# Splitting the contraction of a tuned fp32r feed-forward's up products into two 64-row matmuls with PSUM banks of their own

## The chip, the core and the metric

The kernel runs on one core of one Trainium2 chip. The metric is the device time of one launch in microseconds, the median of three runs. All TensorE work of the feed-forward layers is in fp32r; the six engines that the profile names are PE (matmuls), PEld (the weight loads of PE), DVE (VectorE), ACT (ScalarE), POOL (GpSimd) and SP (SyncE, which here only issues DMAs).

## The reference, cut to what matters

A trunk of two layers over 512 tokens of width 1024. Layer 0 mixes tokens with an RG-LRU, layer 1 with an S5 block; each mixer is followed by a gated feed-forward with a causal convolution of three taps over the tokens. The second of these two feed-forwards is the place of the change:

```python
D_MODEL, SEQ, D_FF, FFN_CONV_W = 1024, 512, 3072, 3

def _conv_ffn(h, w_up, conv_w, conv_b, w_down):
    up = _causal_dwconv(h @ w_up, conv_w, conv_b)
    return (jax.nn.gelu(up[..., :D_FF]) * up[..., D_FF:]) @ w_down

# in reference(), for each layer i
hn = _rmsnorm(h, norm_ffn_g[i])
h = h + _conv_ffn(hn, ffn_w_up[i], ffn_conv_w[i], ffn_conv_b[i], ffn_w_down[i])
```

`h @ w_up` is [512 x 1024] by [1024 x 6144]: 48 tiles of 128 output channels, each contracted over 8 chunks of 128 input channels. All values are float32.

## The kernel before, in words

Channels lie on partitions and tokens on the free axis, so a tile is [128 channels, 512 tokens]. Each float32 operand is kept as a rounded high part and a remainder, both fp32r, and a product of two chunks is three matmuls ("passes") into one PSUM bank: high by high, high by remainder, remainder by high (`mm3`, L213 to L217). Each pass is a weight load of 128 rows by 128 columns and a matmul of 128 rows by 512 columns.

The work is a stream of jobs. A job is one weight tile of [128, 1024] (512 KB): a DMA on SP's queue (L176), its high part by ACT (L188 through L211), its remainder by DVE (L189 through L199), and then 24 passes on PE. `run` (L120) emits jobs in order: two jobs ahead the weight is split, five ahead it is loaded; three raw buffers and three split buffers rotate. What follows a product is put off by `defer` to a later job, at a phase ahead of the weight split (0), behind it (1), ahead of the products (2) or behind them (3).

In the feed-forward (`ffn`, L378) there are six parts of four channel tiles. `up(p)` makes eight tiles, four that go through the gelu (a) and four that gate (g); `down(p - 1)` follows it with four jobs. The order is up(0), up(1), down(0), up(2), down(1), and so on, with down(5) at the end in a form of its own (`final`, L1306), where the products have 256 columns. Of the 48 up tiles the first four (the a tiles of up(0)) go through `group` (L239), contraction outermost; the other 44 go through `product` (L229), contraction innermost, which is 24 passes into one bank, taken by `bank()`. There are two PSUM pools of four banks each, A and B. Up products use A, except for the g tiles of up(0), which use B as the down products do.

One job after a tile's products, `half` (L390) evicts it: `conv_a` (L361) multiplies the bank by the row of 1/rms into a padded buffer on DVE (L363, recorded at L199) and makes the last tap and the bias on ACT (L364, recorded at L211); `conv_b` adds the two other taps on DVE (L368, recorded at L208). Then the gelu on ACT (a tiles), or a product on DVE, a rounded copy on ACT and the remainder on DVE (g tiles).

```python
def mm3(self, ps, wh, wl, xh, xl, start, stop):            # L213
    mm(ps, wh, xh, start=start, stop=False)                # L215
    mm(ps, wh, xl, start=False, stop=False)                # L216
    mm(ps, wl, xh, start=False, stop=stop)                 # L217

def conv_a(self, ps, pad, taps, bias, cv):                 # L361
    self.tt(pad[:, n - 1:n - 1 + S], ps, self.rb, MUL)
    self.act(cv, pad[:, n - 1:n - 1 + S], AF.Identity, scale=taps[n - 1], bias=bias)
```

In the trace the names are those of the tiles: `pa` and `pb` are banks of A and B, `ah` and `al` the parts of the second feed-forward's input, `nh` and `nl` those of its gated activations, `whi` and `wlo` those of the weights.

Of the kernel before, what the change touches and what calls it, by code (L numbers as in the profile page):

```python
# [20 lines left out]
S = 512          # tokens  # L21
D = 1024         # model width
KD = D // P      # chunks of channels
FF = 3072
FP = 4           # ffn chunks in one part
# [3 lines left out]
L = 8            # tokens of one step of the chunked S5 scan  # L29
# [3 lines left out]
NGC = P // GC    # groups in one chunk of channels  # L33
# [20 lines left out]
class Job:  # L54
    """One weight tile's worth of matrix products (or, without src, only a place in the order). The weights
    come as [128, 1024], of which a row is split into a parts; cut: pieces that are loaded and split apart."""
# [10 lines left out]
WARM = 8        # matrix products that raise the clock of the tensor engine before the first data is there  # L67
AHEAD = 2        # jobs between the split of a weight and its use
BG = 5.1         # the vector engine's budget for one job, work in the background included (see cost)


class Trunk:
    def __init__(self, tc, ctx):
# [27 lines left out]
        self.sgn = c.tile([P, 2], F32, name="sgn")   # (+1 top, -1 bottom), (-1 top, +1 bottom)  # L101
# [4 lines left out]
        self.imod = c.tile([P, GC], F32, name="imod")  # 1 where column = partition mod 16  # L106
        self.h = [self.hp.tile([P, S], F32, name=f"h{k}") for k in range(KD)]

# [1 line left out]
    def defer(self, ticks, phase, fn, cost=0.0):  # L110
        """Emit fn that many jobs later; phase 0 before the weight split, 1 after it, 2 before the products,
        3 after them."""
        self.queue.setdefault((self.t + ticks, phase), []).append((fn, cost))
# [54 lines left out]
    def load(self, j, part=None):  # L168
        """DMA of a job's weights, or of one of its pieces."""
        if j.raw is None:  # L170
            j.raw = self.wraw.tile([P, 1024], F32, tag="raw", name="raw")
            j.left = list(range(j.cut))
        n = 1024 // j.cut
        for _ in range(len(j.left) if part is None else 1):
            i = j.left.pop(0)
            self.nc.sync.dma_start(out=j.raw[:, i * n:(i + 1) * n], in_=j.src[:, i * n:(i + 1) * n])  # L176

    def split_weight(self, j, part=None):
        """hi and lo of a job's weights, or of one piece."""
# [38 lines left out]

    def pair(self, role):
        """(hi, lo) tiles of a norm's output (role 0) or of what follows it (role 1); the two pools change  # L220
        roles when self.turn does."""
# [7 lines left out]
    def product(self, w, c, x, bank, post):  # L229
        """128 columns of w^T x (tile c of w, c > 3), contraction innermost; x() gives its (hi, lo) lists."""  # L230
        def emit(wh, wl):
            ps = bank()
            xh, xl = x()
            for k in range(KD):
                self.mm3(ps, wh[:, k, :], wl[:, k, :], xh[k], xl[k], k == 0, k == KD - 1)
# [3 lines left out]
    def group(self, w, x, bank, post):  # L239
        """The first 512 columns (tiles 0 to 3 of w), contraction outermost, so that the last chunks of x may  # L240
        come late."""
# [19 lines left out]
    def norm_begin(self, gain):  # L261
        """gain(k): column of gains for chunk k, or None for the last norm."""
# [3 lines left out]
    def norm_act(self, k):  # L266
        """hi of h * g, squares."""
# [15 lines left out]
    def norm_vec(self, k):  # L283
        """lo of h * g, sum of the squares."""
# [14 lines left out]
    def norm_rsqrt(self):  # L299
        """1/rms of every token as [128 tokens, 4]."""  # L300
# [14 lines left out]
    def norm_bcast(self):  # L315
        """1/rms of the tokens on every partition."""
# [4 lines left out]
    def spread(self, ps, t, r):  # L321
        """Column t of r, a value per token, as a row on every partition."""
# [8 lines left out]
    def norm_tail(self, d=0):  # L331
        """The rest of the norm, spread over the jobs of the next phase's first group."""
# [5 lines left out]
    def residual(self, m, ps, view=lambda h, ps: (h, ps), norm=True, d=1):  # L338
        """h[m] += ps as a post of the running job, with the next norm's part for this chunk."""
# [21 lines left out]
    def conv_a(self, ps, pad, taps, bias, cv):  # L361
        n = len(taps)
        self.tt(pad[:, n - 1:n - 1 + S], ps, self.rb, MUL)  # L363
# [14 lines left out]
    def ffn(self, w_up, w_down, ft, next_gain, before_last=None, last=None):  # L378
# [4 lines left out]
        def half(ps, f, d, then):  # L383
            """conv of one 128-channel tile; then(cv) right behind it."""
# [41 lines left out]
        def up(p):  # L426
# [6 lines left out]
            for f in fs:  # L433
                if p:
                    yield self.product(w_up, f, self.x_now, self.bankA,
                                       lambda ps, f=f: half(ps, f, 1, a_half(f)))
                yield self.product(w_up, FF // P + f, self.x_now, self.bankA if p else self.bankB,
                                   lambda ps, f=f: half(ps, FF // P + f, 1, g_half(f)))
# [31 lines left out]
    def project(self, w, x, next_gain, view=lambda h, ps: (h, ps), turn=0, mid=None):  # L470
        """h += w^T x; mid is emitted half way."""
# [12 lines left out]
    def rglru(self, x, g_first, late_tables, gt, w_in, w_a, w_x, w_out, next_gain, then):  # L484
# [30 lines left out]
        def four(tag, c):  # L515
            """Slice c of a tile for four chunks, whose transcendental functions then are one instruction."""
# [159 lines left out]
    def exp_parts(self, pool, x, n, pre):  # L676
        """x (overwritten, clamped) -> expm1 of the reduced argument, k of 2^k."""
# [16 lines left out]
    def softplus_neg(self, tmp, lam):  # L694
        """-2 and -4 times softplus(-lam) over [128, 8]."""
# [4 lines left out]
        self.ts(v, lam, -1.0, 0.0, op0=MUL, op1=ALU.max)       # max(-lam, 0)  # L700
        self.stt(z, v, -2.0, lam, MUL, SUB)                    # -2 max(-lam,0) - lam = -|lam|
# [3 lines left out]
        self.stt(p, p, 1.0, e, ADD, MUL)                       # exp(-|lam|)  # L705
# [16 lines left out]
    def s5_pre(self, a, log_dt, b, c, d_col):  # L722
        """Matrices and tables of the chunked scan, one chunk of 8 groups at a time, into DRAM: a list of
        (emit, cost on the vector engine). Partitions hold (real | imaginary) x state unless said otherwise."""
        nc, tc = self.nc, self.tc
        G = NG
        self.d_P = self.dr.tile([KD, P, 2304], F32, name="d_P")     # S, four tables of e, R
# [10 lines left out]
        def open_tab():  # L738
            st["tab"] = ExitStack()
            tab = st["tab"].enter_context(tc.tile_pool(name="s5tab", bufs=1))  # L740
            for n in ("pw_r", "pw_s", "pw_n", "pw_m"):   # Re lambda^k, +-Re, -Im, -+Im
# [44 lines left out]
        def s_theta():  # L786
            # theta = ai dt, reduced, halved
# [22 lines left out]
        def s_w():  # L810
            cm, co, si, sn, cs = t("cm"), t("co"), t("si"), v["sn"], v["cs"]
            self.stt(cm, sn, -2.0, sn, MUL, MUL)           # cos - 1
# [5 lines left out]
            # w = (lambda - 1) conj(a) / |a|^2  # L818
# [17 lines left out]
            self.ts(t("wis"), wi, self.sgn[:, 1:2])        # -wi top, +wi bottom  # L836
            # rho8 = mag^8
# [6 lines left out]
        def power_block(re, im, base, lo, n, tmpn):  # L844
            """entries lo+1..lo+n = entry(base) * entries 1..n"""
# [36 lines left out]
        def unit_square():  # L882
            # squares e^{i x}, kept at modulus 1
# [14 lines left out]
        def s_e1t():  # L898
            pi8 = v["pi"][:, :, 0:8]
            power_table(v["e1c"], pi8, v["co"], v["si"], 7)  # L900
            self.ts(v["e1s"], pi8, self.sgn[:, 1:2])       # -sin top, +sin bottom

        def s_e2t():
            e2, e2x = v["e2"], v["e2x"]
            power_table(e2, e2x, v["co"], v["si"], 7)
            # e2 = cos top, sin bottom; e2x = sin top, cos bottom
# [13 lines left out]
        # Bbar and its swapped halves  # L920
# [72 lines left out]
        def c_K(m, R):  # L993
            # K[(l, c), (g, c')], then [(g, c'), (l, c)]
# [58 lines left out]
        def t_move():  # L1053
            # T_g[(j', c'), (j, c)] = K_{j - j'}[c', c]
# [19 lines left out]
    def s5(self, w_in, w_glu, w_out, next_gain):  # L1074
# [19 lines left out]
        def tables(c):  # L1094
            # e^{i 8 theta n}: [cos; sin], then [cos; cos] and [sin; sin]
# [12 lines left out]
        def params2(c):  # L1108
            # the first chunks' matrices wait in tiles that the activations need only later
# [15 lines left out]
        def up(c, ps):  # L1125
            # rows of a chunk are (c, g); tokens in (j, n) order, then to [(j, c), (g, n)] through DRAM
# [397 lines left out]
```

## Time and profile before

| what | value |
|---|---|
| median of 3 runs | 1209.42 us (1209.22 to 1210.38) |
| profiled execution, from its first to its last instruction | 1204.7 us |
| what the median has beyond that span | 4.7 us |
| PE busy | 1190.3 us, 99% of the span, 5616 matmuls |
| PEld busy | 992.3 us, 82% |
| DVE busy | 887.1 us, 74% |
| ACT busy | 525.9 us, 44% |
| mean granted TensorE clock | 0.993 of full speed |

A profile shows when each engine executed something. PE's durations run from a matmul's start to its modelled end and overlap one another, so the step from one start to the next tells what a matmul costs in a stream. The profile states no separate whole time for the profiled execution; its span is set beside the median of the runs.

### The profile page before, as it was taken

To read this page: it belongs to the slowest core of one execution; us is meant where nothing else is said; L and a number is where in the kernel's file an instruction comes from. 1 tells how busy PE (TensorE), PEld (TensorE's weight loads), DVE (VectorE), ACT (ScalarE), POOL (GpSimd) and SP (SyncE) were. 2 spreads that over 40 slices of the span, in tenths; PEclk is the share of its full clock that TensorE was granted. 3 is DMA by queue.
4 is the path that set the end of the run, shared out by engine and by line. 5 is a ranking of instruction groups with operands and counts; after the bars stand their busy time and mean duration, and the time that the engine had idled before them with its cause. 6 is when DMAs were issued, how large, how long until landed. Compare 5 with 4: busy or idle time off the path is not lost.

```text
span 1204.7 us, 14706 instructions
## 1 busy us (share of the span) xinstructions
PE 1190.3 (99%) x5616; PEld 992.3 (82%) x5616; DVE 887.1 (74%) x1469; ACT 525.9 (44%) x711; POOL 18.6 (2%) x35
## 2 busy tenths in 40 slices
PE   9999999999999999999999999999999999999997
PEld 7777888888888888888889888888888888888886
DVE  7899799989989888678597432657766757575765
ACT  5588425424334243436267342524433434242434
POOL 0000000000000000102001000000000000000000
PEclk9999999999999999999989999999999999999998
DMA  7212423247553443457377522223232222223212
GB/s 271 85 56 88 143 88 105 97 121 272 169 159 125 143 142 125 130 192 272 116 217 250 163 99 100 93 95 98 89 104 91 101 95 98 100 92 105 89 70 71
DMA packets 78439, 154.15 MB, mean 128 GB/s; under 512 B 26464, under 2 KB 42224, under 8 KB 78240
## 3 DMA queue, kind: packets, MB, share of 16 engines
q1 hardware_dynamic: 74256, 138.26, 34.8%
q0 software_dynamic: 4112, 14.94, 3.4%
q8 instruction: 44, 0.72, 0.2%
q14 instruction: 27, 0.22, 0.1%
HBM read 131.69 MB, written 23.86 MB: 129 GB/s over the span
## 4 chain that ended last, share of the span: by engine, by line
PE 92%; DVE 4%; ACT 2%; DMA 1%; issue 1%; SPq 0%; DVEq 0%; ACTq 0%
PE pa L215 17%; PE pa L217 17%; PE pa L216 17%; PE pb L215 12%; PE pb L217 12%; PE pb L216 12%; PE py L1184 1%; PE py L1183 1%; PE kps L998 1%; PE pv L1142 1%; DVE wlo L199 1%; PE sps L1033 1%; DMA raw<-in_rg_w_in_dram 1%; DVE xc L208 0%; PE rb L323 0%
## 5 line engine op out<-in xcount | busy, mean ns | idle before, releaser
L211 ACT ACTIVATE whi<-raw 128x1024 fp32r<-128x1024 f32 (+1 forms) x201 | 211.6, 1054 | 372.0 <-PE pa L216 164.0
L199 DVE TENSOR_TENSOR wlo<-raw,whi 128x1024 fp32r<-128x1024 f32 (+1 forms) x201 | 244.7, 1218 | 93.6 <-ACT whi L211 82.1
L215 PE MATMUL pa<-nh,whi 128*128 128x512 f32 x520 | 207.6, 400 | 0.7 <-ACT whi L211 0.7
L217 PE MATMUL pa<-nh,wlo 128*128 128x512 f32 x520 | 202.8, 391 | 0.1
L216 PE MATMUL pa<-nl,whi 128*128 128x512 f32 x520 | 202.3, 389 | 0.0
L215 PE MATMUL pa<-ah,whi 128*128 128x512 f32 x448 | 173.9, 391 | 1.4 <-DVE g L199 1.4
L216 PE MATMUL pa<-al,whi 128*128 128x512 f32 x448 | 174.5, 390 | 0.0
L217 PE MATMUL pa<-ah,wlo 128*128 128x512 f32 x448 | 174.4, 389 | 0.0
L208 DVE SCALAR_TENSOR_TENSOR cv<-pad,t_f,cv 128x512 f32<-128x512 f32 x192 | 142.5, 748 | 3.6 <-ACT cv L211 1.8
L215 PE MATMUL pb<-nh,whi 128*128 128x512 f32 (+1 forms) x344 | 129.0, 375 | 0.0
L217 PE MATMUL pb<-nh,wlo 128*128 128x512 f32 (+1 forms) x344 | 127.8, 371 | 0.0
L216 PE MATMUL pb<-nl,whi 128*128 128x512 f32 (+1 forms) x344 | 127.7, 371 | 0.0
L215 PE MATMUL pb<-ah,whi 128*128 128x512 f32 x320 | 125.4, 392 | 0.0
L217 PE MATMUL pb<-ah,wlo 128*128 128x512 f32 x320 | 124.6, 390 | 0.0
L216 PE MATMUL pb<-al,whi 128*128 128x512 f32 x320 | 124.5, 389 | 0.0
L199 DVE TENSOR_TENSOR pad<-pa,rb 128x512 f32<-128x512 f32 x88 | 60.7, 690 | 78.2 <-PE pa L217 78.0
L199 DVE TENSOR_TENSOR h<-h,pb 128x512 f32<-128x512 f32 (+1 forms) x112 | 72.3, 648 | 61.6 <-PE pb L217 61.2
L215 PEld LDWEIGHTS pa<-nh,whi 128*128 128x128 f32 x520 | 97.6, 188 | 22.5 <-issue 1.7
L217 PEld LDWEIGHTS pa<-nh,wlo 128*128 128x128 f32 x520 | 97.5, 188 | 21.8 <-DVE wlo L199 0.9
L216 PEld LDWEIGHTS pa<-nl,whi 128*128 128x128 f32 x520 | 97.7, 188 | 21.2 <-issue 1.7
L215 PEld LDWEIGHTS pa<-ah,whi 128*128 128x128 f32 x448 | 83.9, 188 | 18.8 <-DVE g L199 1.8
L217 PEld LDWEIGHTS pa<-ah,wlo 128*128 128x128 f32 x448 | 84.1, 188 | 17.6
(280 smaller groups left out, 1488.8 us busy)
## 6 DMA issues: line engine op xcount, KB each, us to landing
raw<-in_ffn_w_up_dram SPq DMA_DIRECT2D x96, 512.0 KB, 3.5
raw<-in_ffn_w_down_dram SPq DMA_DIRECT2D x48, 512.0 KB, 3.5
raw<-in_s_w_glu_dram SPq DMA_DIRECT2D x16, 512.0 KB, 3.5
raw<-in_rg_w_in_dram SPq DMA_DIRECT2D x15, 512.0 KB, 3.4
mS<-d_P SPq DMA_DIRECT2D x8, 640.0 KB, 5.9
raw<-in_rg_w_out_dram SPq DMA_DIRECT2D x8, 512.0 KB, 3.5
d_T<-zero POOLq DMA_DIRECT2D x1, 4096.0 KB, 16.4
d_P<-se SPq DMA_DIRECT2D x16, 256.0 KB, 2.0
```

What stands on the lines that cost most here:

```text
L199: self.last_vec = self.nc.vector.tensor_tensor(out=out, in0=a, in1=b, op=op).ins
L208: self.nc.vector.scalar_tensor_tensor(out, a, s, b, op0, op1)
L211: self.nc.scalar.activation(out, a, func, **kw)
L215: mm(ps, wh, xh, start=start, stop=False)
L216: mm(ps, wh, xl, start=False, stop=False)
L217: mm(ps, wl, xh, start=False, stop=stop)
L998: nc.tensor.matmul(ps[:, g * GC:(g + 1) * GC], R[:, g, 0:8].rearrange("p l c -> p (l c)"), bst[:, g], start=True, stop=True)
L1033: nc.tensor.transpose(ps[:, i * P:(i + 1) * P], Sm[:, i].rearrange("p l c -> p (l c)"), self.ident)
L1142: nc.tensor.matmul(pv[:, g * NCH:(g + 1) * NCH], mS[:, g * P:(g + 1) * P], us[:, g * NCH:(g + 1) * NCH], start=True, stop=True)
L1183: nc.tensor.matmul(o, mT[g // 4][:, gs], us[:, g * NCH:(g + 1) * NCH], start=True, stop=False)
L1184: nc.tensor.matmul(o, mR[g // 4][:, gs], hs[:, g, 0:NCH], start=False, stop=True)
```

## The change

The 44 tiles of the second feed-forward that go through `product` are contracted in two halves. Each pass becomes two matmuls, one over partitions 0 to 63 and one over partitions 64 to 127, each with its own weight load of 64 rows by 128 columns and its own PSUM bank. A tile takes two banks in place of one. At the eviction ACT copies the first bank into `cv`, DVE adds the second bank to it, and the multiplication by the row of 1/rms reads `cv` in place of PSUM. The order of jobs, the loads and everything in the first feed-forward stay as they are. (The diff also drops comments and docstrings from the file; these hunks are left out.)

```diff
+    def mm3_rows(self, pss, wh, wl, xh, xl, start, stop):
+
+        for q, (w, x) in enumerate(((wh, xh), (wh, xl), (wl, xh))):
+            for ps, r in zip(pss, (slice(0, 64), slice(64, 128))):
+                self.nc.tensor.matmul(ps, w[r], x[r], start=start and q == 0, stop=stop and q == 2)
+
...
-    def product(self, w, c, x, bank, post):
+    def product(self, w, c, x, bank, post, rows=False):
         def emit(wh, wl):
-            ps = bank()
+            ps = (bank(), bank()) if rows else bank()
+            mm3 = self.mm3_rows if rows else self.mm3
             xh, xl = x()
             for k in range(KD):
-                self.mm3(ps, wh[:, k, :], wl[:, k, :], xh[k], xl[k], k == 0, k == KD - 1)
+                mm3(ps, wh[:, k, :], wl[:, k, :], xh[k], xl[k], k == 0, k == KD - 1)
             post(ps)
         return Job(w[c], emit, KD)
...
     def conv_a(self, ps, pad, taps, bias, cv):
         n = len(taps)
+        if type(ps) is tuple:
+            self.act(cv, ps[0], AF.Copy)
+            self.tt(cv, cv, ps[1], ADD)
+            ps = cv
         self.tt(pad[:, n - 1:n - 1 + S], ps, self.rb, MUL)
         self.act(cv, pad[:, n - 1:n - 1 + S], AF.Identity, scale=taps[n - 1], bias=bias)
...
-    def ffn(self, w_up, w_down, ft, next_gain, before_last=None, last=None):
+    def ffn(self, w_up, w_down, ft, next_gain, before_last=None, last=None, rows=False):
...
                 if p:
                     yield self.product(w_up, f, self.x_now, self.bankA,
-                                       lambda ps, f=f: half(ps, f, 1, a_half(f)))
+                                       lambda ps, f=f: half(ps, f, 1, a_half(f)), rows)
                 yield self.product(w_up, FF // P + f, self.x_now, self.bankA if p else self.bankB,
-                                   lambda ps, f=f: half(ps, FF // P + f, 1, g_half(f)))
+                                   lambda ps, f=f: half(ps, FF // P + f, 1, g_half(f)), rows)
...
         yield from K.ffn(ffn_w_up[1], ffn_w_down[1], Taps(1), None,
-                         last=lambda w, x: K.final(w, x, lambda k: gt("fin", k), out))
+                         last=lambda w, x: K.final(w, x, lambda k: gt("fin", k), out), rows=True)
```

## Rows read from the trace of the kernel before

**Rows 1.** The page's first part: engine, busy us, share of the span, instructions

```profile
PE 1190.3 (99%) x5616; PEld 992.3 (82%) x5616; DVE 887.1 (74%) x1469; ACT 525.9 (44%) x711; POOL 18.6 (2%) x35
```

**Rows 2.** The page's chain of work that ended last, by engine

```profile
PE 92%; DVE 4%; ACT 2%; DMA 1%; issue 1%; SPq 0%; DVEq 0%; ACTq 0%
```

**Rows 3.** Busy time by stretch: length, then each engine's busy us (instructions), granted clock

```profile
1169.09:1181.97 12.88, 12.88 (x109) 12.87 (x108) 6.91 (x16) 6.45 (x16) 0.00 (x0) 1.00 0.01 1
842.69:886.21 43.52, 43.52 (x193) 36.04 (x192) 32.34 (x41) 20.02 (x25) 0.00 (x0) 1.00 0.29 97
820.93:842.69 21.76, 21.76 (x97) 18.02 (x96) 19.99 (x28) 11.52 (x17) 0.00 (x0) 1.00 0.30 97
1103.81:1147.33 43.52, 43.52 (x193) 36.04 (x192) 29.12 (x36) 18.17 (x22) 0.00 (x0) 1.00 0.28 97
```

**Rows 4.** Groups of instructions in 1103.81 to 1147.33: count | busy us, mean ns | idle before

```profile
L216 PE MATMUL pa<-al,whi 128*128 128x512 f32 x64 | 24.9, 389 | 0.0
...
L216 PEld LDWEIGHTS pa<-al,whi 128*128 128x128 f32 x64 | 12.0, 188 | 2.5
...
L199 DVE TENSOR_TENSOR pad<-pa,rb 128x512 f32<-128x512 f32 x7 | 4.8, 689 | 8.9 <-PE pa L217 8.9
...
L199 DVE TENSOR_TENSOR h<-h,pb 128x512 f32<-128x512 f32 x1 | 0.7, 686 | 2.0 <-PE pb L217 2.0
```

**Rows 5.** Timeline of PE and PEld at 850 us: start, us, instruction

```profile
850.40 0.39 PE L216 MATMUL pa<-al,whi 128*128 128x512 f32 x1
850.40 0.19 PEld L217 LDWEIGHTS pa<-ah,wlo 128*128 128x128 f32 x1
850.63 0.39 PE L217 MATMUL pa<-ah,wlo 128*128 128x512 f32 x1
850.63 0.19 PEld L215 LDWEIGHTS pa<-ah,whi 128*128 128x128 f32 x1
```

**Rows 6.** Timeline of PEld at 661 us, ten weight loads merged: S5 products of 64 columns

```profile
661.12 1.31 PEld L1142 LDWEIGHTS pv<-us,mS 128*128 128x128 f32 x10
662.35 0.19 PEld L1183 LDWEIGHTS py<-us,mT 128*128 128x128 f32 x1
```

**Rows 7.** Copies of a whole PSUM bank by ACT: min/median/max ns, first and last start

```profile
L211 ACT ACTIVATE us<-pa x8: 578/598/601, 697.6 to 733.0; 128x512 f32<-128x512 f32 x8
```

**Rows 8.** Timeline of DVE from 853 to 859.5 us

```profile
853.77 0.69 DVE L199 TENSOR_TENSOR pad<-pa,rb 128x512 f32<-128x512 f32 x1 [1.54 <-PE pa L217]
854.69 1.22 DVE L199 TENSOR_TENSOR wlo<-raw,whi 128x1024 fp32r<-128x1024 f32 x1 [0.22 <-ACT whi L211]
855.83 1.53 DVE L208 SCALAR_TENSOR_TENSOR cv<-pad,t_f,cv 128x512 f32<-128x512 f32 x2
857.40 0.69 DVE L199 TENSOR_TENSOR ge<-ge,cv 128x512 f32<-128x512 f32 x1
858.79 0.69 DVE L199 TENSOR_TENSOR nl<-ge,nh 128x512 fp32r<-128x512 f32 x1 [0.70 <-ACT nh L211]
```

**Rows 9.** Who waited for whom from 842.69 to 1169.09 us: total us, times, longest

```profile
DVE pad L199 <- PE pa L217: 50.2, 24, 3.3
ACT whi L211 <- PE pa L216: 41.7, 39, 4.4
```

**Rows 10.** Timeline of PE where a down block ends and an up block begins

```profile
1103.59 0.39 PE L217 MATMUL pb<-nh,wlo 128*128 128x512 f32 x1
1103.81 0.39 PE L215 MATMUL pa<-ah,whi 128*128 128x512 f32 x1
```

## The prediction, made before the changed kernel was run

> **What bounds the kernel now.** I read the busy shares first, then the chain of waits, then the second feed-forward by stretches, and last single matmuls on the timeline. PE is busy for 99% of the span [rows 1] and makes 92% of the chain that ended last [rows 2]: what TensorE's stream gains or loses, the kernel gains or loses, and other engines count only where they make PE wait. In the stretches of the change PE has no gap at all at a granted clock of 1.00 [rows 3]. The changed passes lie in 820.93 to 842.69 (the g tiles of up(0), 96 passes) and in five stretches like 842.69 to 886.21 (192 passes each, the last is 1103.81 to 1147.33): 96 + 5 x 192 = 1056 passes, which is 44 tiles of 24.
>
> A pass costs 43.52 us / 192 = 226.7 ns from start to start [rows 3]; the 389 ns of a matmul's row and the 188 ns of a load's [rows 4] are longer because they overlap. The timeline shows how: the load for the next pass starts in the same moment as the running matmul, and the next matmul starts 0.23 us later [rows 5]. At the level of 2.4 GHz, which a granted clock of 1.00 stands for, 512 columns take 213.3 ns, so 13.4 ns of each pass are not columns. The last products, of 256 columns, take 12.88 us / 108 = 119.3 ns [rows 3]; 106.7 ns of it are columns, so the rest is 12.6 ns: a fixed price of some 13 ns per load and matmul, not a slower stream. All that splitting could win on PE is this remainder, for every pass still streams 512 columns through both halves of the array. 1056 x 13.4 ns = 14.2 us is the most, a reason that excludes a larger gain.
>
> The Trainium skill, page "TensorE: Matmul & The Clock Gate", Part 3, section "What overlaps and what doesn't", says that a weight load overlaps matmuls in flight only when it goes to other rows of the array. Here loads of all 128 rows run beside matmuls of all 128 rows [rows 5], so the "only" does not hold in this trace; at most the 13 ns could be what such a load can't hide. Taken at its word, the rule would hide them in the changed kernel, which is the first rival below.
>
> **The change part by part.**
>
> *The passes.* A pass becomes two loads and two matmuls of 64 rows each. No row of the trace has a matmul of fewer than 128 rows, so I bound the price. From below: both row tiles stream together and nothing else shows, 213.3 ns, -14.2 us over 1056 passes. From above: they never run together, each costs what a pass costs now, 2 x 226.7 = 453.4 ns, +239.4 us. Between them lie three rows. If each row tile is a stream of its own with the step of today's passes, and the two streams run side by side, a pass stays at 226.7 ns: no change. If the loads go one after the other: ten loads for matmuls of 64 columns take 1.23 us, from 661.12 to 662.35 [rows 6]; the first step is that of the 512-column matmul still running, 0.23 us [rows 5], so the nine others are (1.23 - 0.23) / 9 = 0.111 us each, and two loads fit into 222 ns, just inside a pass. And if the fixed 13.4 ns is paid for each load and matmul in turn although the columns run together, a pass is 213.3 + 26.8 = 240.1 ns, +14.2 us; twice the step of the 256-column products, 238.6 ns, says the same in another way [rows 3].
>
> I take 226.7 ns. It is the row nearest in kind: the same load of 128 columns beside the same stream of 512, with the weights of the next pass loaded behind the columns of this one, only with each stream's rows halved. Two streams in different rows, with different partitions of the operands and different banks, share no operand and no result in the program. Sum of this term: 0.
>
> *The borders.* Ten times PE passes between split and whole products: into the first stretch, five times out to a down block, four times back. Today such a border costs nothing: the step over it is 0.22 us [rows 10]. If the array has to empty at a border, the price is the tail of a matmul beyond its step, 389 - 227 = 162 ns [rows 4], so 0 to 1.6 us in all. I take 1.0, nearer to the tail since nothing in the trace changes the shape of the array.
>
> *The eviction.* Added per tile: an ACT copy of a bank, 0.60 us [rows 7], and a DVE addition of a bank, 0.69 us as for the residual [rows 4]. 44 x 0.60 = 26 us of ACT and 44 x 0.69 = 30 us of DVE, none of it on PE. The multiplication by 1/rms reads SBUF in place of PSUM; its 0.69 us [rows 4] is the same as that of the gated product, which reads SBUF [rows 8], so 0. DVE's load in a usual up stretch goes from 29.12 to 29.12 + 8 x 0.69 = 34.6 of 43.52 us, in the first one from 32.34 to 37.9; in 820.93 to 842.69 three of the split tiles are evicted, 19.99 + 2.1 = 22.1 us against 21.76 [rows 3]. There alone DVE falls behind, by some 0.3 us and the waits for ACT's copy, and the next stretch has 5.6 us to spare. What hides the eviction is the idle time that DVE now spends waiting for PE ahead of it, 50.2 us in all, and ACT's wait ahead of the weight split [rows 9]. If that cover were gone, 44 x 0.69 = 30 us would lie on PE.
>
> *The wait that is added.* In front of DVE's addition stands ACT's copy, and behind it in DVE's queue are the multiplication, the weight's remainder and the taps; behind the copy in ACT's queue is the next weight's high part. Today the multiplication starts 0.2 us after the tile's end and the remainder 0.9 us after that [rows 8]. Both move by some 1.4 us. The weight so split is used two jobs (10.9 us) later and the gated activations from four jobs later on, so nobody on PE waits for them.
>
> *The banks.* A tile takes two of a pool's four banks, so a pair must be free again after one job of 5.44 us (43.52 / 8). It is free at 0.2 + 0.60 + 0.69 = 1.5 us, plus DVE's arrears. 3.9 us are left: 0. Loads from memory and SP's queue are the same.
>
> **Sum.** 0 + 1.0 + 0 + 0 = +1.0 us on the profiled span of 1204.7 us; the median lies 4.7 us above that span, and with the same difference it becomes 1209.4 + 1.0 = 1210.4 us.
>
> **The rivals.** *The fixed price is hidden.* The load of one half passes while the other half streams, so the 13.4 ns vanish. For it: it is a price per load and matmul, not per column. Against it: loads already run wholly beside columns. It gives 213.3 to 222 ns a pass, the upper end being two loads in turn: -14.2 to -5.0 us, and with the borders 1195.3 to 1206 us.
>
> *The fixed price is paid twice.* 240.1 ns a pass, +14.2 us, with the borders 1224 to 1225 us; with an arrear of DVE of a few us on top up to 1229. For it: it comes once per load and matmul, and their number doubles. It decides if it sits where instructions are taken up one after the other, and not in the array.
>
> *The two halves do not run together*, so the change doesn't do what it is built on. Place: PE's queue, at the second matmul of each pass. Price: 226.7 ns per pass, +239.4 us, 1449 us. It decides as soon as the second half's matmul starts over 0.11 us after the first's and the next pass starts only behind both. For it: every matmul in this trace starts when the one before has streamed, and a matmul of half the rows still has 512 columns. Against it: the program gives no reason for one half to wait for the other.
>
> The Trainium skill, page "TensorEngine Tiling (Array Packing)", section "Key Properties", says that row tiles load and multiply independently and that a change of tiling drains the array. By it this last rival falls and the border's price stands; no run here has shown either yet.
>
> **How the numbers follow.** No change: 0.36, the likeliest, with 1209.4 to 1211.0 as its own range. Price hidden: 0.24. Price paid twice: 0.20. Halves one after the other: 0.20, since nothing in the trace has shown two matmuls at once. A measurement of this kernel can tell 0.2% (2.4 us) from no change. So faster 0.24, same 0.36, slower 0.20 + 0.20 = 0.40. The range takes in the first three cases with their bounds, 1196 to 1229 us, and leaves out the last.
>
> **What would show it.** Right: in a stretch of an up block, 192 passes of two matmuls each in 43.5 us; matmuls of 64 rows whose starts come in pairs or interleave at half a pass; PE without gaps; DVE's pad rows now behind ACT's copy, DVE at 34 to 38 us per stretch; ten short gaps at the borders. Price hidden: the stretch shrinks to 41 to 42.6 us. Paid twice: 46 us. One after the other: 87 us, with a step of 227 ns from each matmul to the next. I am wrong about the eviction if PE's first matmul of a tile waits for ACT or DVE.

## The result, and the profile after

The changed kernel takes 1243.62 us (median of 4 runs, 1238.99 to 1247.12) against 1209.32 us for the kernel before in the same sessions: 1.0292 times, 95% interval 1.0258 to 1.0326. It was forecast at 1210.4 us, no change, with a range of 1196 to 1229. The profiled execution has a span of 1237.2 us in a run of 1238.99 us, the fastest of the four.

The page of the changed kernel, its engines and its chain by engine, set beside [rows 1, 2]:

```profile
PE 1201.5 (97%) x6672; PEld 995.7 (80%) x6672; DVE 915.3 (74%) x1513; ACT 545.1 (44%) x755; POOL 18.6 (2%) x35
...
PE 75%; DVE 15%; ACT 6%; issue 2%; DMA 1%; SPq 0%; DVEq 0%; ACTq 0%
```

1056 more matmuls and loads are there (6672 - 5616), and yet PE's busy time grew by 11 us only. The chain of work that ended last moved: DVE and ACT make 21% of it where they made 6%. By stretches (length, then PE, PEld, DVE, ACT and POOL busy us, granted clock, DMA share, GB/s), beside [rows 3]:

```profile
817.87:839.78 21.91, 21.91 (x193) 19.03 (x194) 17.46 (x25) 11.26 (x17) 0.00 (x0) 1.00 0.24 73
839.78:897.14 57.36, 48.95 (x387) 40.02 (x383) 39.58 (x52) 23.80 (x34) 0.00 (x0) 0.94 0.25 74
897.14:919.15 22.01, 22.01 (x98) 17.94 (x97) 16.72 (x22) 7.67 (x11) 0.00 (x0) 1.00 0.37 118
919.15:967.89 48.74, 45.66 (x385) 36.42 (x384) 30.35 (x39) 19.51 (x27) 0.00 (x0) 1.00 0.25 77
```

The g tiles of up(0) cost what they cost (21.91 us for 21.76), and a down block 22.01 for 21.76. The five other up stretches had 43.52 us each; the first now has 57.36, and the other four have 48.74 to 48.76. From the first split tile to the 256-column products the kernel before needs 1169.09 - 820.93 = 348.16 us and this one 1202.11 - 817.87 = 384.24 us, +36.1 us. This length I use for all runs below: what lies ahead of it differs by some us from run to run of the same code.

PE's timeline in such a stretch, and its loads, beside [rows 5]:

```profile
922.02 0.39 PE L223 MATMUL pa<-ah,whi 64*128 64x512 f32 x2
922.25 0.39 PE L223 MATMUL pa<-al,whi 64*128 64x512 f32 x2
...
922.03 0.19 PEld L223 LDWEIGHTS pa<-al,whi 64*128 64x128 f32 x2
```

The two halves run together: a pair of matmuls starts every 0.23 us, the step that one whole pass had, with two loads beside it. So the passes are as forecast; the 5 us per stretch are lost between tiles. Who waited for whom from 817 to 1202 us (total, times, longest), beside [rows 9]:

```profile
ACT cv L211 <- DVE pad L199: 97.8, 45, 4.2
DVE wlo L199 <- ACT whi L211: 60.7, 49, 4.5
...
DVE cv L208 <- ACT cv L211: 34.6, 44, 0.9
...
PE pa L223 <- DVE cv L199: 14.8, 21, 0.9
...
PE pa L223 <- ACT cv L211: 5.8, 6, 4.6
```

PE waits for DVE's addition (`cv` at L199) and ACT's copy, which is to wait for a pair of banks. In its timeline at the start of a tile, the first half's matmul runs alone, for its bank is free when ACT has copied it; the second half's bank waits for the addition:

```profile
947.00 0.40 PE L223 MATMUL pa<-ah,whi 64*128 64x512 f32 x1
948.27 0.50 PE L223 MATMUL pa<-ah,whi 64*128 64x512 f32 x1 [0.88 <-DVE cv L199]
```

DVE's eviction of the up tiles no longer waits for PE; it waits for ACT, and ACT for DVE. The timeline of DVE over two tiles, beside [rows 8], and under it ACT's over one, show why (start, duration, engine, line, tiles; in brackets the wait ahead and what ended it):

```profile
933.58 0.68 DVE L199 TENSOR_TENSOR cv<-cv,pa 128x512 f32<-128x512 f32 x1
934.29 0.69 DVE L199 TENSOR_TENSOR pad<-cv,rb 128x512 f32<-128x512 f32 x1
935.86 1.54 DVE L208 SCALAR_TENSOR_TENSOR cv<-pad,t_f,cv 128x512 f32<-128x512 f32 x2 [0.88 <-ACT cv L211]
...
939.77 1.22 DVE L199 TENSOR_TENSOR wlo<-raw,whi 128x1024 fp32r<-128x1024 f32 x1 [0.26 <-ACT whi L211]
940.92 0.68 DVE L199 TENSOR_TENSOR cv<-cv,pa 128x512 f32<-128x512 f32 x1
...
943.21 1.54 DVE L208 SCALAR_TENSOR_TENSOR cv<-pad,t_f,cv 128x512 f32<-128x512 f32 x2 [0.88 <-ACT cv L211]
946.39 1.23 DVE L199 TENSOR_TENSOR wlo<-raw,whi 128x1024 fp32r<-128x1024 f32 x1 [1.65 <-ACT whi L211]
947.53 0.68 DVE L199 TENSOR_TENSOR cv<-cv,pa 128x512 f32<-128x512 f32 x1
```

```profile
938.16 0.63 ACT L211 ACTIVATE nh<-ge 128x512 fp32r<-128x512 f32 x1 [2.33 <-DVE ge L199]
938.70 1.04 ACT L211 ACTIVATE whi<-raw 128x1024 fp32r<-128x1024 f32 x1
939.64 0.58 ACT L211 ACTIVATE cv<-pa 128x512 f32<-128x512 f32 x1
942.36 0.82 ACT L211 ACTIVATE cv<-pad,t_f 128x512 f32<-128x512 f32 x1 [2.13 <-DVE pad L199]
944.78 0.63 ACT L211 ACTIVATE ge<-cv 128x512 f32<-128x512 f32 x1 [1.60 <-DVE cv L208]
```

The two queues hand one another the work in a ring, a chain that runs from one engine to the other and back once per tile. In the kernel before the order on DVE is multiplication, weight's remainder, taps [rows 8], so ACT makes the last tap beside the remainder. Here the remainder (`wlo`) stands ahead of the addition, nothing is beside ACT's tap, and DVE waits 0.88 us for it; and on ACT the weight's high part (`whi`, 1.04 us) stands behind the gelu or the rounded copy and ahead of the bank's copy, so DVE waits 1.65 us for gelu and high part. From addition to addition it is 940.92 - 933.58 = 7.34 us for one tile and 947.53 - 940.92 = 6.61 us for the next, 6.98 on average, though DVE is busy for only 4.1 to 5.5 us of that; PE needs 5.45 us for a tile. The order is set when the kernel is built. It came out so only where the split passes and the new eviction stand together: in two of the experiments below, the split passes with the eviction of before and whole passes with the new eviction, the build kept the order of before. Why it did not keep it here is open. I call the changed kernel's order the late order.

In the first stretch the lag of the four g tiles of up(0) comes on top: their pairs are in B, so PE does not feel it at once. It falls due at the third tile of up(1), which needs the pair of the first back: ACT copies that pair's first bank only at 854.93 us. This wait for ACT's copy, the longest of the rows above, lasts 4.6 us, and behind it PE comes back at half clock (columns as above):

```profile
850.57:855.50 4.93, 0.39 (x4) 0.00 (x0) 3.33 (x5) 2.60 (x4) 0.00 (x0) 0.98 0.23 89
855.50:862.00 6.50, 5.86 (x25) 4.27 (x27) 3.90 (x6) 2.76 (x5) 0.00 (x0) 0.50 0.28 81
```

Of the 4.93 us of the first row PE is busy for 0.39. Behind it the granted clock is 0.50, the level of 1.2 GHz, for 6.5 us. With both, the long wait and the half clock, the stretch takes 57.36 us where the four others take 48.74 to 48.76.

The 36.1 us by these rows: PE's gaps in the five up stretches are 57.36 - 48.95 = 8.4 us in the first and 12.2 in the four others (48.74 - 45.66 = 3.08 in the one shown), together 20.6 us, which is what the two PE rows of the waits add up to (14.8 + 5.8). Its busy time there is longer than that of a stretch without gaps (43.61, in the first experiment below) by 5.3 us in the first, where the half clock falls, and by some 2.1 in each of the others, 13.7 in all: the tail of a matmul ahead of each gap, a first step behind it of 0.33 us in place of 0.23, and first matmuls that run without their partner all count as busy. The borders make the rest: the down blocks take 0.16 to 0.25 us more each.

### The profile page after: what moved, and what is told of

It reads as the page before. It is cut to its first block, busy times and chain, and to the rows that moved or that the text cites. A ratio compares the mean times of both kernels' runs of the same rounds, so it can differ in the third digit from the quotient of the medians.

```text
span 1237.2 us, 16905 instructions
## 1 busy us (share of the span) xinstructions
PE 1201.5 (97%) x6672; PEld 995.7 (80%) x6672; DVE 915.3 (74%) x1513; ACT 545.1 (44%) x755; POOL 18.6 (2%) x35
## 4 chain that ended last, share of the span: by engine, by line
PE 75%; DVE 15%; ACT 6%; issue 2%; DMA 1%; SPq 0%; DVEq 0%; ACTq 0%
PE pa L215 11%; PE pb L215 11%; PE pb L217 11%; PE pb L216 11%; PE pa L217 11%; PE pa L216 11%; PE pa L223 4%; DVE wlo L199 4%; DVE cv L208 4%; ACT whi L211 3%; ACT cv L211 2%; DVE cv L199 2%; DVE pad L199 2%; PE py L1195 1%; PE py L1194 1%
## 5 line engine op out<-in xcount | busy, mean ns | idle before, releaser
L199 DVE TENSOR_TENSOR wlo<-raw,whi 128x1024 fp32r<-128x1024 f32 (+1 forms) x201 | 244.4, 1216 | 145.3 <-ACT whi L211 133.9
L215 PE MATMUL pa<-nh,whi 128*128 128x512 f32 x520 | 207.5, 399 | 1.4 <-ACT whi L211 1.4
L217 PE MATMUL pa<-nh,wlo 128*128 128x512 f32 x520 | 202.6, 390 | 0.0
L216 PE MATMUL pa<-nl,whi 128*128 128x512 f32 x520 | 202.3, 389 | 0.0
L223 PE MATMUL pa<-ah,whi 64*128 64x512 f32 x640 | 175.1, 396 | 20.6 <-DVE cv L199 14.8
L223 PE MATMUL pa<-al,whi 64*128 64x512 f32 x640 | 170.2, 393 | 0.0
L223 PE MATMUL pa<-ah,wlo 64*128 64x512 f32 x640 | 167.8, 390 | 0.0
L223 PEld LDWEIGHTS pa<-ah,whi 64*128 64x128 f32 x640 | 95.2, 186 | 43.2 <-DVE cv L199 22.3
L215 PE MATMUL pb<-nh,whi 128*128 128x512 f32 (+1 forms) x344 | 128.8, 374 | 0.0
L217 PE MATMUL pb<-nh,wlo 128*128 128x512 f32 (+1 forms) x344 | 127.2, 370 | 0.0
L216 PE MATMUL pb<-nl,whi 128*128 128x512 f32 (+1 forms) x344 | 127.1, 369 | 0.0
L211 ACT ACTIVATE cv<-pad,t_f 128x512 f32<-128x512 f32 x96 | 77.7, 812 | 111.1 <-DVE pad L199 110.9
L215 PEld LDWEIGHTS pa<-nh,whi 128*128 128x128 f32 x520 | 97.6, 188 | 22.9 <-issue 1.7
L216 PEld LDWEIGHTS pa<-nl,whi 128*128 128x128 f32 x520 | 97.7, 188 | 21.3 <-issue 1.7
L217 PEld LDWEIGHTS pa<-nh,wlo 128*128 128x128 f32 x520 | 97.6, 188 | 20.9
L215 PE MATMUL pb<-ah,whi 128*128 128x512 f32 x288 | 113.0, 392 | 0.0
L217 PE MATMUL pb<-ah,wlo 128*128 128x512 f32 x288 | 112.2, 390 | 0.0
L216 PE MATMUL pb<-al,whi 128*128 128x512 f32 x288 | 112.1, 389 | 0.0
L223 PEld LDWEIGHTS pa<-ah,wlo 64*128 64x128 f32 x640 | 95.1, 186 | 12.2
L223 PEld LDWEIGHTS pa<-al,whi 64*128 64x128 f32 x640 | 93.5, 186 | 11.1
```

Source lines behind the costliest of these rows:

```text
L199: self.last_vec = self.nc.vector.tensor_tensor(out=out, in0=a, in1=b, op=op).ins
L211: self.nc.scalar.activation(out, a, func, **kw)
L223: self.nc.tensor.matmul(ps, w[r], x[r], start=start and q == 0, stop=stop and q == 2)
```

## The experiments

The theory: the split matmuls cost no more than the borders; the loss is the ring over ACT and DVE, much slower than PE because of its order, and felt because a tile holds two of four banks. The rivals: the split matmuls, the added 56 us of ACT and DVE work as such, the banks as such, the order as such. All diffs are cut, and against the changed kernel unless the text says otherwise. Apart from the order changed back, each experiment is a single run; the kernel before took 1203.07 to 1214.17 us in 13 runs beside five of them and 1210.03 us in one run beside the other three. Totals a few us apart say little at that scatter, so I compare the stretches.

**One bank evicted.** The split passes with the eviction of the kernel before; the lower 64 rows' part of the sum is computed and not read.

```diff
         if type(ps) is tuple:
-            self.act(cv, ps[0], AF.Copy)
-            self.tt(cv, cv, ps[1], ADD)
-            ps = cv
+            ps = ps[0]
```

> The changed kernel with its 64-row matmuls and both banks, but the eviction of the kernel before: the first bank alone is read, ACT's copy and DVE's addition are left out, so the output lacks the contraction over the lower 64 rows of each chunk. Theory (the time went into the eviction's place in the queues, the row tiles cost nothing but the borders): up stretches of 192 passes 43.5 to 44 us without a gap on PE, 1209 to 1212 us in all. Rival 1 (the split matmuls themselves are slower): the stretches stay near 48.7 us, 1235 us or more. Rival 2 (the pairs of banks alone, two tiles in flight in place of four, hold PE up): gaps ahead of a tile's first matmul remain although the eviction is short, 1220 us or more.

1214.44 us in one run. The stretches:

```profile
848.40:892.01 43.61, 43.61 (x386) 35.78 (x382) 33.08 (x43) 20.01 (x26) 0.00 (x0) 1.00 0.35 108
...
914.02:957.79 43.77, 43.77 (x386) 35.90 (x385) 29.13 (x36) 18.14 (x23) 0.00 (x0) 1.00 0.32 97
```

PE has no gap, and an up stretch takes 43.61 to 43.77 us for 43.52. The whole length is 1177.02 - 826.49 = 350.53 us, +2.4. The total lies 2.4 us over what I expected, but this run was already 5.6 us late where the split begins (826.49 for 820.93). Neither the split matmuls nor the pairs of banks make the loss by themselves; the ten borders cost 0.24 us each. The run changes more than the eviction's length, though: the build put DVE's queue back into the order of before (multiplication at 925.25, remainder at 926.17, taps at 927.32 us). So it does not tell the order from the added work; the next two runs do.

**The order changed back**, with all instructions of the changed kernel. One edge puts the weight's high part behind the bank's copy on ACT, the other puts the weight's remainder behind the multiplication by 1/rms on DVE:

```diff
-            self.act(hi[:, c], j.raw[:, c], AF.Copy)
-            self.tt(lo[:, c], j.raw[:, c], hi[:, c].bitcast(F32), SUB)
+            with self.tc.issue_after(self.behind_act) if self.behind_act is not None else nullcontext():
+                self.act(hi[:, c], j.raw[:, c], AF.Copy)
+            with self.tc.issue_after(self.behind_vec) if self.behind_vec is not None else nullcontext():
+                self.tt(lo[:, c], j.raw[:, c], hi[:, c].bitcast(F32), SUB)
...
             self.act(cv, ps[0], AF.Copy)
+            self.behind_act = self.last_act
             self.tt(cv, cv, ps[1], ADD)
             ps = cv
+            self.behind_vec = True
         self.tt(pad[:, n - 1:n - 1 + S], ps, self.rb, MUL)
+        if self.behind_vec is True:
+            self.behind_vec = self.last_vec
```

> The changed kernel whole, with the issue order alone changed: ACT makes the next weight's high part behind the copy of the first bank, and DVE the weight's remainder behind the multiplication by 1/rms, as in the kernel before, so that ACT's last tap again runs beside the remainder. Same instructions, same durations. Theory (order): a tile's ring over ACT and DVE falls from 6.6 (a) and 7.3 us (g) to some 5.4 and 6.1, the lag over eight tiles is below the 3.9 us that a pair of banks leaves; stretches 43.5 to 44.5 us, 1210 to 1215 us. Rival 1 (the added 30 us of DVE and 26 us of ACT are what costs, whatever the order): 1235 us or more. Rival 2 (the split matmuls): 1235 us or more.

1210.54 us (10 runs) against 1208.45 us (13 runs): 1.0015 times, interval 0.9994 to 1.0036. The loss is gone. DVE's timeline and two stretches:

```profile
928.82 0.68 DVE L203 TENSOR_TENSOR cv<-cv,pa 128x512 f32<-128x512 f32 x1
929.53 0.69 DVE L203 TENSOR_TENSOR pad<-cv,rb 128x512 f32<-128x512 f32 x1
930.14 1.22 DVE L203 TENSOR_TENSOR wlo<-raw,whi 128x1024 fp32r<-128x1024 f32 x1
931.28 1.53 DVE L212 SCALAR_TENSOR_TENSOR cv<-pad,t_f,cv 128x512 f32<-128x512 f32 x2
934.00 0.69 DVE L203 TENSOR_TENSOR cv<-cv,pa 128x512 f32<-128x512 f32 x1 [1.18 <-ACT cv L215]
...
843.84:888.92 45.08, 44.81 (x387) 35.74 (x383) 37.35 (x50) 22.94 (x32) 0.00 (x0) 1.00 0.31 94
...
910.92:954.69 43.77, 43.77 (x385) 35.90 (x385) 32.77 (x43) 20.73 (x28) 0.00 (x0) 1.00 0.27 85
```

No wait stands between the addition and the taps. A turn of the ring is now 934.00 - 928.82 = 5.18 us, and 928.82 - 922.78 = 6.04 us for the tile before, 5.61 on average. That is still over PE's 5.45, but by 0.16 us a tile in place of 1.5, and eight tiles of that fit into the time that a pair of banks leaves. Only the first stretch, with four g tiles ahead of its eight, keeps 1.5 us; the whole length is 1173.92 - 821.92 = 352.00 us, +3.8, of which 2.4 are the borders.

**Whole passes, two banks.** Even chunks go into one bank, odd ones into the other, with the copy and the addition of the changed kernel:

```diff
-                mm3(ps, wh[:, k, :], wl[:, k, :], xh[k], xl[k], k == 0, k == KD - 1)
+                if rows:
+                    self.mm3(ps[k % 2], wh[:, k, :], wl[:, k, :], xh[k], xl[k], k < 2, k > KD - 3)
+                else:
+                    mm3(ps, wh[:, k, :], wl[:, k, :], xh[k], xl[k], k == 0, k == KD - 1)
```

> No row tiles: whole 128-row passes as before, even chunks of the contraction into the first bank of a pair and odd ones into the second, and the eviction of the changed kernel (copy, addition). Here the build by itself puts the copy ahead of the weight's high part and the remainder behind the multiplication. Theory (order): no more than in the run with the order changed, 1209 to 1215 us, though the added instructions and the two banks are all there. Rival 1 (the added work or the pairs of banks): as slow as the changed kernel, 1235 us or more. Rival 2 (the split matmuls): 1209 us, which this run alone does not tell from the theory.

1209.78 us. The whole length is 1172.89 - 824.73 = 348.16 us, that of the kernel before to the last digit, with DVE at 33.13 us in a stretch:

```profile
911.77:955.29 43.52, 43.52 (x193) 36.04 (x192) 33.13 (x43) 21.48 (x30) 0.00 (x0) 1.00 0.28 92
```

The added 44 copies and 44 additions, and two tiles in flight in place of four, cost nothing in the order of before, which the build kept here.

**Whole passes, late order.** The run above with edges that give ACT's and DVE's queues the changed kernel's order: the high part behind gelu or rounded copy, the remainder behind the last tap or the activation's remainder, and copy and addition behind these. Two deferred pieces also change their phase: the eviction goes behind the weight split, and the activation's remainder ahead of it:

```diff
-            self.act(hi[:, c], j.raw[:, c], AF.Copy)
-            self.tt(lo[:, c], j.raw[:, c], hi[:, c].bitcast(F32), SUB)
+            with self.tc.issue_after(self.gate[0]) if self.gate else nullcontext():
+                self.act(hi[:, c], j.raw[:, c], AF.Copy)
+            self.last_whi = self.last_act
+            with self.tc.issue_after(self.gate[1]) if self.gate else nullcontext():
+                self.tt(lo[:, c], j.raw[:, c], hi[:, c].bitcast(F32), SUB)
+            self.last_wlo = self.last_vec
...
-            self.act(cv, ps[0], AF.Copy)
-            self.tt(cv, cv, ps[1], ADD)
+            with self.tc.issue_after(self.last_whi):
+                self.act(cv, ps[0], AF.Copy)
+            with self.tc.issue_after(self.last_wlo):
+                self.tt(cv, cv, ps[1], ADD)
...
-            self.defer(d, 0, a, 0.6)
+            self.defer(d, 1 if type(ps) is tuple else 0, a, 0.6)
...
-                self.defer(1, 1, lo, 0.6)
+                self.defer(1, 0 if rows else 1, lo, 0.6)
```

> The run before with one thing changed: edges of issue order put ACT's and DVE's queues into the order that the changed kernel has (high part of the weight behind the gelu or the rounded copy, bank copy behind it; remainder ahead of the addition). Whole 128-row passes. Theory (order): the ring of 6.6 and 7.3 us is back, PE waits for DVE's addition from the third or fourth tile of a stretch on; stretches 48 to 49.5 us, 1232 to 1245 us. Rival (split matmuls needed for the loss): 1209 to 1215 us.

1245.30 us, 0.3 us over the top of what I expected, with no split matmul in it. DVE's additions, and the waits from 827.63 to 1200 us:

```profile
879.77 0.68 DVE L204 TENSOR_TENSOR cv<-cv,pa 128x512 f32<-128x512 f32 x1
...
886.39 0.68 DVE L204 TENSOR_TENSOR cv<-cv,pa 128x512 f32<-128x512 f32 x1
...
893.73 0.68 DVE L204 TENSOR_TENSOR cv<-cv,pa 128x512 f32<-128x512 f32 x1
...
DVE cv L213 <- ACT cv L216: 33.2, 39, 0.9
...
PE pa L220 <- ACT cv L216: 14.3, 11, 4.7
...
PE pb L220 <- ACT whi L216: 7.0, 9, 1.3
```

The ring is back, with 6.62 and 7.34 us from addition to addition, and so are DVE's waits of 0.9 us. With them most of the loss is back: the whole length is 1203.64 - 827.63 = 376.01 us, +27.9 where the changed kernel has +36.1. It isn't the changed kernel in all else. PE waits for ACT's copy, and not for the addition as I expected: the second bank is needed three passes after the first. The build also drew some matmuls of the down blocks into the stretches, so the stretches can't be set side by side, and 7.0 us of PE's waits are for weights.

**The halves apart.** First all 24 passes over the upper rows, then all over the lower ones:

```diff
-                mm3(ps, wh[:, k, :], wl[:, k, :], xh[k], xl[k], k == 0, k == KD - 1)
+                if not rows:
+                    mm3(ps, wh[:, k, :], wl[:, k, :], xh[k], xl[k], k == 0, k == KD - 1)
+            for i, r in enumerate((slice(0, 64), slice(64, 128)) if rows else ()):
+                for k in range(KD):
+                    self.mm3(ps[i], wh[r, k, :], wl[r, k, :], xh[k][r], xl[k][r], k == 0, k == KD - 1)
```

> The changed kernel with its 64-row matmuls in another sequence: of each tile first the 24 passes over partitions 0 to 63, then the 24 over 64 to 127, in place of the two halves of a pass next to each other. Same loads, same matmuls, same banks. Theory (matmuls are taken up in program order, and two run together only where neighbours in the queue use different rows): no two run together, each step is some 227 ns, 1056 x 227 ns = +239 us, which also hides the eviction: 1445 to 1455 us. Rival (each half of the array takes its own next matmul from anywhere in the queue): steps in pairs as in the changed kernel, 1209 to 1245 us.

1386.12 us: far slower, as the theory says, but 60 us faster than it says. A stretch takes 76.03 us (956.65 to 1032.68), 198 ns per matmul. PE's timeline where the upper rows of a tile follow the lower rows of the one before:

```profile
965.80 0.39 PE L216 MATMUL pa<-al,whi 64*128 64x512 f32 x1
966.03 0.39 PE L217 MATMUL pa<-ah,wlo 64*128 64x512 f32 x1
966.03 0.60 PE L215 MATMUL pa<-ah,whi 64*128 64x512 f32 x2
966.37 0.50 PE L216 MATMUL pa<-al,whi 64*128 64x512 f32 x2
966.60 0.49 PE L217 MATMUL pa<-ah,wlo 64*128 64x512 f32 x2
966.83 0.39 PE L215 MATMUL pa<-ah,whi 64*128 64x512 f32 x1
```

In the program the last chunk's L215, L216, L217 come ahead of the other half's L215, L216, L217. They start as two L215, two L216, two L217. So three matmuls of the next half start ahead of matmuls that precede them in the program: that part of the theory, a strict order, falls, and that two halves meet only when they are near in the queue stands. The three that run beside others save 24 x (226.7 - 198) ns = 0.69 us for each half of a tile, and 88 x 0.69 = 61 us make up the 60. The price of not meeting is near 227 ns a step; the third rival's price was right, its condition was not.

**Eight banks.** Each pair takes a bank of either pool, so four tiles can be in flight:

```diff
-            ps = (bank(), bank()) if rows else bank()
+            ps = (self.bankA(), self.bankB()) if rows else bank()
```

> The changed kernel with each pair made of one bank of either pool, so that four tiles can be in flight in place of two; the order in ACT's and DVE's queues stays the changed kernel's. Theory (the ring over ACT and DVE is slower than PE, 6.6 and 7.3 us a tile against 5.45; banks only say how long PE can run ahead): the lag of 8 x 1.5 = 12 us in a usual stretch is just inside the 3.9 + 10.9 us that four pairs leave, but the weights, which are split in the same ring two jobs ahead, come late in their place; part of the loss stays, 1213 to 1232 us, with waits of PE for the weight's parts. Rival (two tiles in flight are the cause): 1209 to 1212 us, no wait.

1257.20 us, 25 us over the top of what I expected and slower than the changed kernel. An up stretch and the down block behind it:

```profile
927.87:971.63 43.76, 43.76 (x385) 35.94 (x384) 27.29 (x34) 16.89 (x23) 0.00 (x0) 1.00 0.25 75
971.63:1001.51 29.88, 25.35 (x98) 19.78 (x96) 20.09 (x27) 10.38 (x14) 0.00 (x0) 0.89 0.31 103
...
PE pb L215 <- DVE cv L199: 4.5, 2, 3.6
```

The up stretch is free of gaps, as the theory has it: PE runs ahead of the ring. But the lag is then whole when the down block begins, whose products need a bank of B that late tiles still hold; it takes 29.88 us for 22.01, 4.5 us of it in the two waits of the last row (from 927.87 to 1001.51 us), and the granted clock is 0.89. I had left out that the down products share these banks. So more banks moved the wait and did not remove it, with a ring that lags 1.5 us a tile. The run doesn't settle whether four tiles in flight would have been enough, since it also takes B from the down products.

**Half of the order.** The edge on DVE alone, without the one on ACT (this diff is against the run with the order changed back):

```diff
-            self.behind_act = self.last_act
```

> The changed kernel with one half of the order changed: the weight's remainder behind the multiplication by 1/rms on DVE, while on ACT the weight's high part stays ahead of the bank copy. Theory: DVE's wait for the last tap (0.88 us per tile) goes, the high part of 1.05 us stays in the ring, which is 6.3 (a) and 7.0 us (g); stretches some 46 us, 1218 to 1232 us, between the changed kernel and the run with both. Rival 1 (the remainder's place alone is the cause): 1209 to 1213 us. Rival 2 (the high part's place alone is the cause): 1238 to 1246 us.

1226.11 us. A stretch takes 45.65 us; the whole length is 1189.26 - 821.22 = 368.04 us, +19.9 where the changed kernel has +36.1 and both edges have +3.8. In this sequence each half of the order makes about half of the loss (the edge on ACT alone was not run): with the high part still ahead of the copy, DVE waits 2.13 us for the copy ahead of every second addition and 0.74 us ahead of the others.

**The order alone.** The kernel before (one bank per tile, whole passes, no copy, no addition) with the late order; the edges and the two moved phases are those of the late order above, with the multiplication by 1/rms behind the remainder.

> The kernel before with the changed kernel's queue order alone: whole 128-row passes, one bank per tile and four tiles in flight, no copy and no addition, but the weight's high part behind the gelu or rounded copy on ACT and its remainder ahead of the multiplication by 1/rms on DVE. Theory: the ring without the copy's and the addition's part is some 5.9 us (a tiles) and 6.6 us (g tiles), still over PE's 5.44, so a stretch of eight tiles lags by some 6 us, which four banks cover; nothing or little on PE, 1208 to 1216 us: order, added work and pairs are needed together. Rival (the order alone makes the loss): 1230 us or more.

1212.13 us. The ring is there:

```profile
939.73 0.69 DVE L204 TENSOR_TENSOR pad<-pa,rb 128x512 f32<-128x512 f32 x1
941.30 1.54 DVE L213 SCALAR_TENSOR_TENSOR cv<-pad,t_f,cv 128x512 f32<-128x512 f32 x2 [0.89 <-ACT cv L216]
...
946.36 0.68 DVE L204 TENSOR_TENSOR pad<-pa,rb 128x512 f32<-128x512 f32 x1
...
952.25 0.68 DVE L204 TENSOR_TENSOR pad<-pa,rb 128x512 f32<-128x512 f32 x1
```

6.63 and 5.89 us a tile, 6.26 on average and over PE's 5.44, so each stretch still lags by 8 x 0.8 = 6.6 us; but with four tiles in flight only the first stretch and the down block behind it show it. The whole length is 1174.79 - 821.10 = 353.69 us, +5.5. So the late order alone costs 5.5 us, pairs of banks with the short eviction 2.4, all of it at the borders, pairs with the added instructions in the order of before nothing, and all three together 27.9 us with whole passes and 36.1 with split ones. Whether the late order needs both others or only one of them is not shown: the late order with pairs and without the added instructions was not run, and the eight banks don't tell.

## Why the prediction was wrong, point by point

**The passes: right.** 226.7 ns was taken for a pass of two halves; a stretch of 192 of them takes 43.61 to 43.77 us where nothing else waits, 227 to 228 ns with the borders in. The fixed 13 ns are neither hidden (first rival) nor paid twice (second rival). The rule of the Trainium skill, page "TensorEngine Tiling (Array Packing)", section "Key Properties", that row tiles load and multiply independently agrees with the trace: a pair of matmuls and a pair of loads every 0.23 us.

**The borders: right in kind, too small.** 1.0 us was taken and 1.6 bounded; the run with one bank evicted measures 2.4 us for ten. The step from a split to a whole pass shows more than the tail of one matmul. That the array drains there, as the same section of the Trainium skill says, fits with it.

**The added wait: the step that failed.** I wrote that both DVE's multiplication and the weight's remainder "move by some 1.4 us" and that "nobody on PE waits for them". That took the order in the queues of [rows 8] as given. The order was another one in the changed kernel, and with it ACT's tap and high part no longer ran beside DVE's work but between it: 6.98 us from addition to addition, where PE needs 5.45. With the order put back it is 5.61 us, and 32 of the 36 us are gone.

**The banks: failed with it.** "It is free at 0.2 + 0.60 + 0.69 = 1.5 us, plus DVE's arrears. 3.9 us are left" is the sum for one tile whose copy starts when its products end. In the ring the copy starts when the tile before is through gelu or rounded copy and the next weight's high part is made, and the arrears are not 0.3 us once but 6.98 - 5.45 = 1.5 us with every tile. 3.9 us are used up after three tiles; from then on PE runs at the ring's pace.

**The eviction's cover: counted in the wrong coin.** I set 34.6 us of DVE work against 43.52 us. The measured run has less: 30.35 us busy in 48.74, with six of the eight additions inside the stretch and the others in the down block. Busy time said nothing of the waits between two queues; the wait rows of before, DVE's 50.2 us for PE [rows 9], were cover only as long as ACT and DVE did not wait for one another. "I am wrong about the eviction if PE's first matmul of a tile waits for ACT or DVE" is what happened: 21 waits for DVE's addition and 6 for ACT's copy in the rows above.

None of the cases that I gave a chance had this in it: of ACT and DVE the range held a few us of arrears and no more. The 0.40 for a slower kernel belonged to two causes that did not come, so that it did come out slower is no support for them.

## What to carry to other kernels

When a change lengthens a chain that runs to and fro between two in-order engines, add up one turn of the ring (durations and waits, in the order in which the queues will hold them) and compare it with the bound engine's time per tile; the busy shares don't show it. Then multiply the difference by the tiles in a row and set it against the time that the buffers leave: here 0.16 us a tile was covered and 1.5 us was not. Where the order is made at build time, it is part of the change: look at it in the built kernel, and fix by an edge what must stay beside what. Here the row split of a contraction that already fills the array gave TensorE nothing and took a second bank, so the eviction got less time for more work.

## What the runs showed of the hardware that was not expected

Matmuls of different rows can start out of program order: three of the next half start between the last three of the half before it, worth 0.69 us per half tile. The Trainium skill, page "TensorE: Matmul & The Clock Gate", Part 3, section "What overlaps and what doesn't", has matmuls start and end strictly in program order; the trace of the halves apart differs, and the measurement decides. A change between 64-row and 128-row matmuls cost 0.24 us. And a stretch of 4.93 us in which PE was busy for 0.39 was followed by 6.5 us at a granted clock of 0.50.
